# Swapping which token half leads at the layer barriers of a two-layer hybrid encoder step

## The chip, the cores and the metric

One core of one Trainium2 chip runs the whole program. The metric is device time in microseconds (us) of one execution; the times of several executions are given as a median. "The profile" is one execution, recorded by the hardware profiler. Engines are named PE (TensorE, its matmuls; PEld its weight loads), DVE (VectorE), ACT (ScalarE), POOL (GpSimd) and SP (SyncE, whose queue issues nearly all DMAs here).

## The reference, cut to what matters

640 tokens (512 of a prompt and 8 x 16 of running streams) of width 1024 pass through two layers. What is around the change:

```python
x = x + rmsnorm(merged @ w_out, g_post_mix)           # end of the mixing sub-layer
f = rmsnorm(x, g_pre_ffn) @ w_gate_up
f = (silu(f[..., :2816]) * f[..., 2816:]) @ w_down
x = x + rmsnorm(f, g_post_ffn)                        # end of the layer
# next layer: h = rmsnorm(x, g_pre_mix); u = h @ w_in
```

A norm over the 1024 channels needs every output of the projection before it, and every product behind it needs the whole norm. These two places, after `w_out` and after `w_down`, are the barriers of a layer. All arithmetic is fp32: weights and activations are split into a high and a low part, and each product is three matmuls.

## The kernel before, in words

Channels lie on the 128 partitions, tokens in the free dimension. The 640 token columns are worked in two halves (`HALF`, L27): half 0 has 256 columns, half 1 has 384. A `Unit` (L218) is one output tile of 128 channels: its weights (8 tiles of 128x128 for `w_out` and `w_gu`, 7 for a part of `w_down`) are loaded by SP as `raw` and split by ACT (`wh`) and DVE or POOL (`wl`); POOL does it for `w_in`. `run` (L244) issues three matmuls for each weight tile on one half into a PSUM tile `pg` (four buffers, L93) and calls the unit's own evacuation. So a unit of 8 tiles has 24 matmuls in each half.

Most units run half 0 and then half 1 in a row. At a barrier this is changed by `add_halves` (L314): pass A runs all units on one half, pass B the same units on the other. The last `keep` units keep their weights from A and go first in B; the others load theirs again. `barrier` (L325) puts the eight units of `w_out`, or of the last part of `w_down`, in this order: pass A on half 0, then the norms of half 0 as a task in lane "bar", pass B on half 1, then the norms of half 1 as a task in lane "bar2". Lane "bar" is finished before the next units are issued. The units behind the barrier (twelve of `w_gu`, L1418, or twelve of `w_in`, L1402) run as two passes too: A on half 0, whose norm is finished by then, with the norms of half 1 beside it, and B on half 1; lane "bar2" is finished ahead of their first B unit.

A task is a generator whose stages are issued one at a time, about one after each unit (`pump`, L272). The norms at a barrier (`bar_mix` L1301, `bar_ffn` L1343) consist of `postnorm` (L413) and `prenorm` (L387). In order of the tiles they write:
- `cs`: PE sums the squares over channels; SP loads the eight tiles `xl` of the residual stream;
- nine small DVE instructions on 2 or 3 columns (a square root and a reciprocal, the last writes `ry`), and PE spreads the result over partitions (`rb`);
- `mo<-mo,pk,rb` and `mo<-mo,xl` (`dn` at the layer's end): eight scalings and eight additions of the residual on DVE; SP stores the eight tiles to `xd`;
- `psq`: eight squares on ACT and seven additions on DVE;
- the second `cs`, nine small instructions, second `rb`;
- `ht<-mo,pk,rb`: eight scalings on DVE; `hh` (ACT) and `hl` (DVE): the split in two parts, which the matmuls of the next units read.

The evacuation of a `w_out` unit is on ACT (L1297 and the square at L410) with an addition `acc<-acc,sq` on DVE; that of a `w_down` unit is an addition on DVE (L140) with the same square and `acc`. A gate unit of `w_gu` is evacuated by a Tanh on ACT (`ft<-pg`, L1314) and `fg<-ft,pg` on DVE (L140), an up unit by `fg<-fg,pg` on DVE and the split `fh`, `fl`. Short tiles (`xl`, `psq`, `ht`, `sq`, `acc`, `ft`, `fg`) share 11 buffers of the pool `hf` (L87).

The framework decides the final order on each engine with a timeline of its own: earlier issued instructions have priority, later ones fill gaps, so an instruction can stand a little ahead of or behind its place in the code. The engines then work their queues in this order.

There are five such places in the program: the start of layer 0 (only norms, half 0 first), the barrier after `w_out` in layers 0 and 1, the barrier between the layers, and the end of layer 1 (L1427), where pass A already runs on half 1 and B on half 0 and nothing but the last norm follows.

Of the kernel before, what the change touches and what calls it, by code (L numbers as in the profile page):

```python
# [72 lines left out]
KEEP_W = (3, 4, 4, 4)  # L73
# [3 lines left out]
def emit(tc, ctx, I, O):  # L77
# [20 lines left out]
    def nm(s):  # L98
        uid[0] += 1
        return f"{s}_{uid[0]}"  # L100

    def blk(shape, s="b", dt=F32):
        return bpool.tile(shape, dt, tag="b", name=nm(s))
# [35 lines left out]
    def stt(o, a, s, b, op0, op1):  # L139
        V.scalar_tensor_tensor(o, a, s, b, op0=op0, op1=op1)  # L140
# [34 lines left out]
    def colsum(sq, n):  # L175

        ps = psb([P, 24], "cs")
        for j in range(n):
            mm(ps[:, j:j + 1], sq[:, j * P:(j + 1) * P], C["ones"], True, True)
        return ps  # L180
# [75 lines left out]
    lanes = {n: deque() for n in ("bar", "bar2", "attn", "ssd", "yn", "convp", "conv", "sc")}  # L256
# [26 lines left out]
    def flush(lane):  # L283
        stuck = 0
        while lanes[lane]:
            if step(lane) or not lanes[lane]:
                stuck = 0
                continue
            stuck += 1
            if stuck > 500:  # L290
                raise RuntimeError("lane is blocked: " + lane)
            for other in ("sc", "convp", "conv"):
                if other != lane:
                    step(other)
# [5 lines left out]
    def trim(flush_all=False):  # L300
        while pending:
            u, lag = pending[0]
            if not flush_all and len(pending) - 1 < lag:
                return
            actions.append(("B", u, 1))
            pending.popleft()
# [7 lines left out]
    def add_halves(us, keep, first=0, between=None):  # L314

        trim(True)
        for i, u in enumerate(us):
            u.drop = i < len(us) - keep
            actions.append(("A", u, first))
        if between:  # L320
            add_hook(between)
        for u in us[len(us) - keep:] + us[:len(us) - keep]:
            actions.append(("B", u, 1 - first))

    def barrier(units, keep, norms, first):  # L325

        add_halves(units, keep, 0, lambda: lanes["bar"].append(norms(0)))
        add_hook(lambda: lanes["bar2"].append(norms(1)))
        add_hook(lambda: flush("bar"))
        first.before = lambda: flush("bar2")  # L330

    def add_hook(f):
        actions.append(("H", f, None))
# [12 lines left out]
    def layer(l):  # L346
        L = {}
# [20 lines left out]
        def par(n, j):  # L368
            o = _PK[n][0]
            return L["pk"][:, o + j:o + j + 1]  # L370
# [69 lines left out]


        def ev_krdt(ps, half, c):
            if half == 0:
                L["raw0"] = blk([P, NT], "raw0")
            act(L["raw0"][:, c], ps, AF.Identity, bias=par("dt_bias", 0))

# [81 lines left out]

        def ev_lora(key, j, n, gname):
            def ev(ps, half, c):  # L530
                if half == 0:
                    L[key, j] = blk([P, NT], key)
                nc.scalar.copy(L[key, j][:, c], ps)
                sq_acc(key, j, half, ps)
                if j == n - 1:
                    if half == 0:
                        L[key + "n"] = [(blk([P, NT], key + "h", F32R), blk([P, NT], key + "l", F32R)) for _ in range(n)]
                    lanes["bar" if n == 2 else "bar2"].append(task_lora(key, n, gname, half))
            return ev

        def task_lora(key, n, gname, half):
            c, nch = HALF[half], HCH[half]
            for _ in range(YL):
                yield
            ps = colsum(L.pop(("sq", key, half)), nch)
            yield
            y = rsqrt(ps, nch, 1.0 / (n * P))
            yield
            rb = bcast(y, nch)
            for j in range(n):  # L550
                t = L[key, j]
                stt(t[:, c], t[:, c], par(gname, j), rb, ALU.mult, ALU.mult)
                split(L[key + "n"][j][0][:, c], L[key + "n"][j][1][:, c], t[:, c])
            if half == 1 and key == "lat":

                lown = lpool.tile([P, 2, P], F32, tag="lown", name=nm("lown"))
                for j in range(n):
                    dma(O["lat"][l, j], L[key, j])
                    G.tensor_copy(lown[:, j, :], L[key, j][:, SEQ:])
                L["lown"] = lown  # L560
            yield
# [284 lines left out]

        def ev_glu_b(j):
            def ev(ps, half, c):
                if half == 0:
                    L["pp", j] = blk([P, 30 + SEQ], "pp")  # L850
                    L["sp", j] = hf(NB * (30 + DS), "sp").rearrange("p (b t) -> p b t", b=NB)
                    G.memset(L["pp", j][:, :30], 0.0)
                    dma(L["sp", j][:, :, :30], I["state_conv"][l, j])
                pp, sp = L["pp", j], L["sp", j]
                t = hf(HW[half], "gt")
                act(t, ps, AF.Tanh, scale=0.5)
                a = L["ga", j, half]

                if half == 0:
                    stt(pp[:, 30:286], t, 1.0, a, ALU.add, ALU.mult)  # L860
                else:
                    stt(pp[:, 286:542], t[:, :256], 1.0, a[:, :256], ALU.add, ALU.mult)
                    stt(sp[:, :, 30:], t[:, 256:].rearrange("p (b t) -> p b t", t=DS), 1.0,
                        a[:, 256:].rearrange("p (b t) -> p b t", t=DS), ALU.add, ALU.mult)
            return ev
# [423 lines left out]

        def wout(m):  # L1290
            def ev(ps, half, c):
                if half == 0:
                    if m == 0:
                        L["mo"] = [None] * 8
                    L["mo"][m] = blk([P, NT], "mo")

                nc.scalar.mul(L["mo"][m][:, c], ps, 0.5)  # L1297
                sq_acc("mo", m, half, ps, 0.5)
            return Unit(I["w_out"][l, m], 8, lambda k: L["mg"][k], ev)

        def bar_mix(half):  # L1301
            sq = yield from postnorm("mo", L["mo"], half, "g_post_mix", xin, xd)
            if half == 0:
                new_h()
            yield
            yield from prenorm(L["mo"], sq, half, "g_pre_ffn")
# [4 lines left out]
        def gu(j):  # L1311
            def ev_g(ps, half, c):
                t, f = hf(HW[half], "ft"), hf(HW[half], "fg")
                act(t, ps, AF.Tanh, scale=0.5)  # L1314
                stt(f, t, 1.0, ps, ALU.add, ALU.mult)
                L["fg", j, half] = f

            def ev_u(ps, half, c):
                if half == 0:
                    L["f", j] = (blk([P, NT], "fh", F32R), blk([P, NT], "fl", F32R))  # L1320
                f = L["fg", j, half]
                tt(V, f, f, ps, ALU.mult)
                split(L["f", j][0][:, c], L["f", j][1][:, c], f)
            return [Unit(I["w_gu"][l, 2 * j], 8, h_rhs, ev_g), Unit(I["w_gu"][l, 2 * j + 1], 8, h_rhs, ev_u)]
# [18 lines left out]
        def bar_ffn(half):  # L1343
            sq = yield from postnorm("dn", L["dn"], half, "g_post_ffn", xd, O["y"] if last else xd, not last)
            if not last:
                nxt = layers[l + 1]
                if half == 0:
                    nxt["load_params"]()
                    nxt["new_h"]()
                yield  # L1350
                yield from nxt["prenorm"](L["dn"], sq, half, "g_pre_mix")
# [26 lines left out]
        def schedule():  # L1378
# [12 lines left out]
            def z(g):  # L1391
# [3 lines left out]
            first = ([wu("krdt", ev_krdt, done_krdt)]  # L1395
                     + [wu(f"kv{j}", ev_lora("lat", j, 2, "g_kv")) for j in range(2)]
                     + [wu(f"q{j}", ev_lora("uq", j, 3, "g_q")) for j in range(3)] + glu(0) + g1[:4])
            if l == 0:
                barrier([], 0, first_norm, first[-KEEP_W[0]])
            else:  # L1400
                barrier([layers[l - 1]["down"](2, m) for m in range(8)], KEEP_W[3], layers[l - 1]["bar_ffn"], first[-KEEP_W[0]])
            add_halves(first, KEEP_W[0])  # L1402
            add_units(g1[4:5])
            add_hook(lambda: (flush("bar"), flush("bar2")))
            add_units([k_unit(p) for p in range(4)] + [VUnit(I["w_uv"][l], 2, None, None)])
# [9 lines left out]
            add_units([mix_ssm(m) for m in range(8)])  # L1415
            us = [u for j in range(6) for u in gu(j)]
            barrier([wout(m) for m in range(8)], KEEP_W[1], bar_mix, us[-KEEP_W[2]])
            add_halves(us, KEEP_W[2])  # L1418
            for g in range(3):
                for j in GROUPS[g]:  # L1420
                    if j >= 6:
# [19 lines left out]
    done = 0  # L1441
# [3 lines left out]
    for i, (k, u, half) in enumerate(actions):  # L1445
# [3 lines left out]
        if i in pos:  # L1449
            for n in loads[done:pos[i] + 3]:  # L1450
                actions[n][1].load()
            done = max(done, pos[i] + 3)
# [163 lines left out]
```

## Time and profile before

| what | value |
|---|---|
| median of 3 runs | 2757.91 us (2756.06 to 2759.37) |
| the profiled execution's own time | 2758.69 us |
| its span, first to last instruction | 2756.9 us |
| mean granted clock of TensorE | 0.983 of full speed |
| PE busy | 2654.8 us, 96% of the span |
| DVE / ACT / POOL busy | 56% / 40% / 29% |

The span is what the engines' records cover; 1.8 us of the execution's own time lie around it. Matmuls overlap one another in the records, so a busy PE is one that has matmuls in flight; what is lost there shows as PE idle time and as time at the lower clock.

### The profile page before, as it was taken

To read this page: it belongs to the slowest core of one execution; us is meant where nothing else is said; L and a number is where in the kernel's file an instruction comes from. 1 tells how busy PE (TensorE), PEld (TensorE's weight loads), DVE (VectorE), ACT (ScalarE), POOL (GpSimd) and SP (SyncE) were. 2 spreads that over 40 slices of the span, in tenths; PEclk is the share of its full clock that TensorE was granted. 3 is DMA by queue.
4 is the path that set the end of the run, shared out by engine and by line. 5 is a ranking of instruction groups with operands and counts; after the bars stand their busy time and mean duration, and the time that the engine had idled before them with its cause. 6 is when DMAs were issued, how large, how long until landed. Compare 5 with 4: busy or idle time off the path is not lost. (4 is left out here: it accounts for less than half of the span.)

```text
span 2756.9 us, 47456 instructions
## 1 busy us (share of the span) xinstructions
PE 2654.8 (96%) x17652; PEld 2563.2 (93%) x17652; DVE 1550.5 (56%) x3382; ACT 1092.5 (40%) x2437; POOL 812.4 (29%) x796
## 2 busy tenths in 40 slices
PE   7999998999999899999999899999999998999998
PEld 7999887899999899999989899888999998999997
DVE  6364758565476732333674648676555666323336
ACT  5535453443334432222455354544433344322222
POOL 5554553544430000000055544645544200000000
PEclk9999999999999999999999999999999999999999
DMA  6443242534644422222454433344436344322224
GB/s 185 148 150 105 74 133 92 157 118 133 210 150 134 161 80 74 74 80 72 128 179 145 137 92 103 114 132 134 141 115 224 122 153 131 91 74 69 81 73 130
DMA packets 248536, 337.81 MB, mean 123 GB/s; under 512 B 52464, under 2 KB 139056, under 8 KB 248304
## 3 DMA queue, kind: packets, MB, share of 16 engines
q1 hardware_dynamic: 246720, 333.75, 39.1%
q8 instruction: 139, 2.28, 0.3%
q10 hardware_dynamic: 1584, 1.02, 0.1%
q14 instruction: 93, 0.76, 0.1%
HBM read 268.73 MB, written 65.94 MB: 121 GB/s over the span
## 5 line engine op out<-in xcount | busy, mean ns | idle before, releaser
L121 PE MATMUL pg<-hh,wh 128*128 128x256 f32 (+1 forms) x3296 | 1045.7, 318 | 26.9 <-DVE fg L140 18.2
L121 PE MATMUL pg<-hl,wh 128*128 128x256 f32 (+1 forms) x3296 | 1038.4, 315 | 5.1 <-DVE hl L137 5.1
L121 PE MATMUL pg<-hh,wl 128*128 128x256 f32 (+1 forms) x3296 | 1029.6, 313 | 0.0
L137 POOL TENSOR_TENSOR wl<-raw,wh 128x512 fp32r<-128x512 f32 (+2 forms) x364 | 513.0, 1415 | 1171.0 <-ACT wh L143 1124.5
L143 ACT CAST wh<-raw 128x512 fp32r<-128x512 f32 (+1 forms) x696 | 423.6, 610 | 850.1 <-PE pg L121 749.9
L121 PEld LDWEIGHTS pg<-hh,wh 128*128 128x128 f32 x3296 | 628.4, 191 | 36.5 <-DVE fg L140 18.6
L121 PEld LDWEIGHTS pg<-hl,wh 128*128 128x128 f32 x3296 | 628.2, 191 | 13.8 <-DVE hl L137 6.0
L121 PEld LDWEIGHTS pg<-hh,wl 128*128 128x128 f32 x3296 | 627.8, 191 | 6.0 <-issue 4.0
L137 DVE TENSOR_TENSOR wl<-raw,wh 128x512 fp32r<-128x512 f32 x332 | 224.3, 677 | 337.8 <-ACT wh L143 336.1
L121 PE MATMUL pg<-fh,wh 128*128 128x256 f32 (+1 forms) x648 | 200.4, 310 | 0.0
L121 PE MATMUL pg<-fl,wh 128*128 128x256 f32 (+1 forms) x648 | 200.3, 309 | 0.0
L121 PE MATMUL pg<-fh,wl 128*128 128x256 f32 (+1 forms) x648 | 200.2, 309 | 0.0
L140 DVE SCALAR_TENSOR_TENSOR cv<-pp,pk,cv 128x512 f32<-128x512 f32 x184 | 157.3, 855 | 2.6 <-POOL cv L137 2.6
L121 PEld LDWEIGHTS pg<-fh,wl 128*128 128x128 f32 x648 | 121.9, 188 | 0.0
L121 PEld LDWEIGHTS pg<-fl,wh 128*128 128x128 f32 x648 | 121.9, 188 | 0.0
L121 PEld LDWEIGHTS pg<-fh,wh 128*128 128x128 f32 x648 | 121.8, 188 | 0.0
L140 DVE SCALAR_TENSOR_TENSOR sa<-pd,pk,sa 128x664 f32<-128x664 f32 x96 | 104.9, 1092 | 20.3 <-ACT sa L985 19.5
L137 POOL TENSOR_TENSOR cv<-cv,cvt 128x640 f32<-128x640 f32 x56 | 88.9, 1587 | 81.8 <-ACT cvt L896 72.0
L140 DVE SCALAR_TENSOR_TENSOR cv<-sp,pk,cv 128x128 f32<-128x128 f32 x184 | 93.2, 506 | 0.0
L137 DVE TENSOR_TENSOR fg<-fg,pg 128x256 f32<-128x256 f32 (+1 forms) x88 | 42.7, 487 | 83.7 <-PE pg L121 83.4
L143 ACT CAST fh<-fg 128x256 fp32r<-128x256 f32 (+1 forms) x88 | 40.3, 460 | 111.6 <-DVE fg L137 108.5
L137 DVE TENSOR_TENSOR acc<-acc,sq 128x256 f32<-128x256 f32 (+1 forms) x96 | 59.9, 625 | 37.0 <-ACT sq L410 35.4
(307 smaller groups left out, 4419.2 us busy)
## 6 DMA issues: line engine op xcount, KB each, us to landing
raw<-in_w_in SPq DMA_DIRECT2D x284, 256.0 KB, 2.8
raw<-in_w_gu SPq DMA_DIRECT2D x208, 256.0 KB, 2.7
raw<-in_w_down SPq DMA_DIRECT2D x72, 256.0 KB, 2.7
raw<-in_w_mix SPq DMA_DIRECT2D x64, 256.0 KB, 3.1
ma<-gd SPq DMA_DIRECT2D x48, 320.0 KB, 4.1
raw<-in_w_out SPq DMA_DIRECT2D x48, 256.0 KB, 2.9
gd<-gs SPq DMA_DIRECT2D x48, 192.0 KB, 2.3
hb<-in_state_ssm SPq DMA_DIRECT2D x64, 128.0 KB, 3.3
```

The source lines that it names most:

```text
L121: nc.tensor.matmul(ps, l, r, start=a, stop=b)
L137: eng.tensor_tensor(o, a, b, op=op)
L140: V.scalar_tensor_tensor(o, a, s, b, op0=op0, op1=op1)
L143: nc.scalar.copy(hi, src)
```

## The change

At the two `w_out` barriers and at the barrier between the layers, pass A now runs on half 1 (384 columns) and pass B on half 0 (256 columns); the norms of half 1 come first and those of half 0 second, and the two passes of the units behind the barrier are turned round in the same way. The start of layer 0 keeps its order by an argument, and the end of layer 1 had the new order already. The other edits make buffers be allocated by whichever half comes first.

```diff
-    def barrier(units, keep, norms, first):
+    def barrier(units, keep, norms, first, lead=1):
 
-        add_halves(units, keep, 0, lambda: lanes["bar"].append(norms(0)))
-        add_hook(lambda: lanes["bar2"].append(norms(1)))
+        add_halves(units, keep, lead, lambda: lanes["bar"].append(norms(lead)))
+        add_hook(lambda: lanes["bar2"].append(norms(1 - lead)))
...
         def ev_krdt(ps, half, c):
-            if half == 0:
+            if "raw0" not in L:
                 L["raw0"] = blk([P, NT], "raw0")
...
-                if half == 0:
+                if (key, j) not in L:
                     L[key, j] = blk([P, NT], key)
...
-            if half == 1 and key == "lat":
+            L[key, "done"] = L.get((key, "done"), 0) + 1
+            if L[key, "done"] == 2 and key == "lat":
...
-                if half == 0:
-                    if m == 0:
-                        L["mo"] = [None] * 8
+                if "mo" not in L:
+                    L["mo"] = [None] * 8
+                if L["mo"][m] is None:
                     L["mo"][m] = blk([P, NT], "mo")
...
             sq = yield from postnorm("mo", L["mo"], half, "g_post_mix", xin, xd)
-            if half == 0:
+            if half == 1:
                 new_h()
...
-                if half == 0:
+                if half == 1:
                     nxt["load_params"]()
                     nxt["new_h"]()
...
-                barrier([], 0, first_norm, first[-KEEP_W[0]])
+                barrier([], 0, first_norm, first[-KEEP_W[0]], 0)
...
-            add_halves(first, KEEP_W[0])
+            add_halves(first, KEEP_W[0], 0 if l == 0 else 1)
...
-            add_halves(us, KEEP_W[2])
+            add_halves(us, KEEP_W[2], 1)
```

## Rows read from the trace of the kernel before

**Rows 1.** The page, part 1: busy time of each engine.

```profile
PE 2654.8 (96%) x17652; PEld 2563.2 (93%) x17652; DVE 1550.5 (56%) x3382; ACT 1092.5 (40%) x2437; POOL 812.4 (29%) x796
```

**Rows 2.** Waits of PE: total us, times, longest us.

```profile
PE pg L121 <- DVE fg L140: 18.2, 2, 9.1
...
PE pg L121 <- DVE hl L137: 5.1, 4, 1.7
...
PE pg L121 <- ACT sq L410: 2.5, 1, 2.5
```

**Rows 3.** Windows, first `w_out` barrier: pass B to restart, then the pass behind.

```profile
core 0: us, PE busy (x) PEld busy (x) DVE busy (x) ACT busy (x) POOL busy (x), PEclk, DMA share, GB/s
861.34:898.57 37.23, 35.79 (x213) 35.59 (x211) 24.16 (x67) 17.84 (x43) 0.00 (x0) 1.00 0.42 128
898.57:916.81 18.24, 18.24 (x153) 18.04 (x153) 14.15 (x37) 7.96 (x16) 0.00 (x0) 1.00 0.64 217
916.81:925.90 9.09, 0.00 (x0) 0.00 (x0) 9.09 (x20) 4.80 (x11) 0.00 (x0) 0.73 0.78 260
925.90:932.00 6.10, 6.10 (x32) 6.10 (x32) 3.80 (x10) 2.10 (x5) 0.00 (x0) 0.56 0.35 121
```

**Rows 4.** Windows, second `w_out` barrier: the stall in the pass behind it.

```profile
2279.79:2288.89 9.10, 0.00 (x1) 0.01 (x1) 9.10 (x20) 5.63 (x13) 0.00 (x0) 0.67 0.78 259
```

**Rows 5.** Windows, barrier between the layers: A, B to restart, then `w_in` pass A.

```profile
1328.46:1348.61 20.15, 20.15 (x170) 20.15 (x170) 14.65 (x30) 11.45 (x23) 0.00 (x0) 1.00 0.62 183
1348.61:1386.76 38.15, 34.00 (x193) 33.39 (x192) 27.22 (x73) 16.22 (x35) 7.74 (x6) 0.94 0.45 141
...
1406.77:1409.31 2.54, 0.00 (x0) 0.00 (x0) 2.54 (x5) 2.54 (x8) 1.39 (x1) 0.97 1.00 361
1409.31:1431.04 21.73, 21.68 (x169) 21.50 (x170) 20.90 (x46) 13.66 (x31) 16.20 (x13) 0.93 0.65 197
```

**Rows 6.** ScalarE and VectorE around the first stall: start, us, engine, operation.

```profile
921.47 2.17 ACT L382 ACTIVATE psq<-mo 128x384 f32<-128x384 f32 x5
...
925.44 0.74 DVE L140 SCALAR_TENSOR_TENSOR fg<-ft,pg 128x256 f32<-128x256 f32 x2
```

**Rows 7.** End of layer 1, 384 columns first: pass A's window, then the chain's timeline.

```profile
2691.13:2720.76 29.63, 29.63 (x171) 29.63 (x171) 16.45 (x30) 12.06 (x23) 0.00 (x0) 1.00 0.58 171
...
2725.57 0.72 PE L121 MATMUL cs<-c_ones,acc 128*128 128x1 f32 x6
...
2729.44 0.18 DVE L194 RECIPROCAL ry<-rt 128x3 f32<-128x3 f32 x1
...
2731.90 0.83 PE L121 MATMUL rb<-c_ident,ry 128*128 128x128 f32 x6
...
2732.77 4.29 DVE L140 SCALAR_TENSOR_TENSOR dn<-dn,pk,rb 128x384 f32<-128x384 f32 x8
```

**Rows 8.** DVE groups by form, 898.57 to 946 us: the norm of 384 columns.

```profile
L137 DVE TENSOR_TENSOR mo<-mo,xl 128x384 f32<-128x384 f32 x8 | 4.2, 551 | 0.0
L137 DVE TENSOR_TENSOR psq<-psq,psq 128x384 f32<-128x384 f32 x7 | 3.6, 549 | 0.0
```

**Rows 9.** DVE groups by form, 861.34 to 898.57 us: beside pass B.

```profile
L137 DVE TENSOR_TENSOR wl<-raw,wh 128x512 fp32r<-128x512 f32 x9 | 6.2, 689 | 7.3 <-ACT wh L143 7.3
L137 DVE TENSOR_TENSOR acc<-acc,sq 128x384 f32<-128x384 f32 x6 | 3.3, 554 | 1.1 <-ACT sq L410 0.9
...
L140 DVE SCALAR_TENSOR_TENSOR ht<-mo,pk,rb 128x256 f32<-128x256 f32 x8 | 3.2, 476 | 0.4 <-PE rb L121 0.4
...
L137 DVE TENSOR_TENSOR mo<-mo,xl 128x256 f32<-128x256 f32 x8 | 2.8, 417 | 0.0
```

**Rows 10.** Timeline of PE, between the layers: the second sum and its spreading.

```profile
1378.08 0.50 PE L121 MATMUL cs<-c_ones,psq 128*128 128x1 f32 x4
1381.85 1.20 PE L121 MATMUL rb<-c_ident,ry 128*128 128x128 f32 x4 [2.46 <-DVE ry L194]
```

**Rows 11.** DVE groups by form, 1386.76 to 1413 us, between the layers.

```profile
L137 DVE TENSOR_TENSOR dn<-dn,xl 128x384 f32<-128x384 f32 x8 | 7.4, 988 | 0.0
```

More of the change, by code (lines that the diff above doesn't have):

```diff
@@ L535, in ev @@
                 if j == n - 1:
-                    if half == 0:
+                    if key + "n" not in L:
                         L[key + "n"] = [(blk([P, NT], key + "h", F32R), blk([P, NT], key + "l", F32R)) for _ in range(n)]
@@ L848, in ev @@
             def ev(ps, half, c):
-                if half == 0:
+                if ("pp", j) not in L:
                     L["pp", j] = blk([P, 30 + SEQ], "pp")
@@ L1302, in bar_mix @@
             sq = yield from postnorm("mo", L["mo"], half, "g_post_mix", xin, xd)
-            if half == 0:
+            if half == 1:
                 new_h()
@@ L1318, in ev_u @@
             def ev_u(ps, half, c):
-                if half == 0:
+                if ("f", j) not in L:
                     L["f", j] = (blk([P, NT], "fh", F32R), blk([P, NT], "fl", F32R))
@@ L1346, in bar_ffn @@
                 nxt = layers[l + 1]
-                if half == 0:
+                if half == 1:
                     nxt["load_params"]()
```

## The prediction

> **What bounds the kernel now.** I read the page first: TensorE is busy for 96% of the span [rows 1], so the change can only win or lose in the time when it is not, and in time at the lower clock. PE's waits come next: the largest wait of matmuls that stands at the places of this change is the one for `fg`, 18.2 us in two pieces; `hl` has 5.1 us, `sq` one piece of 2.5 us [rows 2]. The windows put them on the barriers.
>
> At a `w_out` barrier pass B (384 columns) and the restart behind it take 37.23 us [rows 3]. At the end of layer 1 a pass of 168 matmuls of 384 columns takes 29.63 us [rows 7], 0.176 us each, so 192 take 33.9 us; only 3.3 us of the 37.23 are not matmuls of that pass (four short sums and spreadings, and the wait for `hl`). The norm of the 256-column half is hidden. The loss comes behind it: after 18.24 us of the next pass TensorE stands for 9.09 us, and 9.10 us in the other layer [rows 3, 4]. There the norm of the 384-column half holds DVE and ACT: the Tanh that frees PSUM waits behind `psq` on ACT, and `fg` comes at 925.44 us [rows 6]. With four PSUM buffers full, PE stops. The clock falls: the 6.10 us behind the stall ran at a mean granted clock of 0.56, which is 2.7 us lost [rows 3].
>
> [...]
>
> **The change part by part.** No instruction is added or removed; per layer the same columns, splits, loads and norms run. Two things are swapped: which norm lies in which cover, and how long the covers are. The three moved places are the two `w_out` barriers and the one between the layers. All terms are against the profiled execution, 2758.69 us (span 2756.9 and 1.8 around it); the median is 0.8 us lower.
>
> *The second norm gets 384-column cover.* In the pass behind the barrier PE ran 144 matmuls (six units) before it stopped. At 0.176 us these last 25.4 us, where they took 18.24 us with the sums between them. The stall ended 27.3 us after the restart (925.90 less 898.57, [rows 3]). The norm of 256 columns is shorter: 23 DVE instructions of the burst lose some 0.134 us each (551 against 417 ns, [rows 8, 9]), 3.1 us, so PSUM is freed about 24.2 us after the restart, ahead of the 25.4 us. I take the whole 9.09 and 9.10 us as gone, and between the layers the 2.54 us with its 1.5 us of clock, since there too six units pass before the wait.
>
> *The first norm loses its cover.* It now runs 384 columns beside a pass B of 256. That pass lasts 20.15 us for 168 matmuls [rows 5], so 23.0 us for 192. The end of layer 1 has this order already and gives the first part of the chain: from the end of pass A at 2720.76 us to `rb` at 2731.90 us are 11.1 us, and 0.9 us more to the first scaling [rows 7]. Then DVE has 4.3 us of scalings [rows 7], 4.2 us of additions and 3.6 us of square sums [rows 8]: 12.1 us. Between them stand weight splits and `acc`: in today's pass B 6.2 and 3.3 us in 37.23 us [rows 3, 9], a quarter of the time. The bounds are none and 3.1 us; I take 2.0, nearer to the upper one, because B units now follow each other faster. From the second sum to its spreading I take the 3.8 us between the layers, where PE idles too [rows 10], and from there to the restart 4.9 us (1381.85 to 1386.76, [rows 5, 10]) and 1.1 us for eight longer scalings (4.29 against 3.2 us, [rows 7, 9]). Sum: 11.1 + 0.9 + 12.1 + 2.0 + 3.8 + 6.0 = 35.9 us from the end of pass A to the restart.
>
> At `w_out` this is 12.9 us beyond the matmuls of pass B, where it was 3.3: 9.6 us lost against 9.1 won, +0.5 us at each barrier. The half-clock stretch behind the stall I leave as it is, since one stall of this length takes the place of another; it may move by 2 us either way. Between the layers it is 15.8 us against 8.5, 7.3 us lost against 2.5 and 1.5 won: +3.3 us. In all 2 x 0.5 + 3.3 = +4.3 us: 2763.0 on the profiled execution, 2762.2 beside the median; I say 2762.
>
> *Edits costed at nothing.* Pass A at `w_out` now begins with the half that the units before it finished last. At the end of layer 1 the same turn exists and its window is busy throughout, 29.63 of 29.63 us [rows 7]; if the cover is too short, the last tile's split is late by one or two DVE instructions, about 1 us a barrier. On SP the `xl` loads and `xd` stores of the first norm are larger, and raw weights of the next units are queued behind stores that wait for DVE; their units cannot start before the restart anyway, so the stall hides that, and without that cover it would cost a few us more. The B passes behind the barriers (256 columns now) reload weights for most units: DVE needs two splits of 0.69 us [rows 9] and its evacuation in some 2.8 us of a unit, and today's pass A does the same at this width. In the `w_in` units POOL splits; today's pass A of 256 columns has PE busy for 21.68 of 21.73 us beside it [rows 5].
>
> [...] Between the layers the residual additions of 384 columns took 988 ns each, against 551 ns behind `w_out`, where POOL is idle [rows 8, 11]; POOL was busy for 16.20 of 21.73 us in the window behind [rows 5]. [...]
>
> **The rivals.** *The first norm's chain is shorter than its parts* (faster). In the last barrier `ry` was ready at 2729.62 us, 2.3 us before `rb` was issued [rows 7]: the order on PE held it back. If the new order doesn't, if nothing breaks into the burst (2.0) and if the second sum takes only its short instructions (some 2.5 instead of 3.8), each chain loses 5.6 us, three times 16.8: 2745. Half of it gives 2753.6. For it: the unused 2.3 us. Against it: DVE has weight splits to do in any pass B.
>
> *The second norm still stalls* (slower). The margin above is 1.2 us. It decides at the point where the second norm's squares end more than 25.4 us after the restart. DVE may owe work by then: the nine splits (6.2 us, [rows 9]) compete with a longer first norm. With 5 us more, PE stands for 3.8 us and loses 2.7 us of clock at both `w_out` barriers: +13.0, 2775. For it: the thin margin. Against it: `acc` of the second half is complete long before the restart, so its sum can start early.
>
> *POOL stands in the way of the first norm between the layers* (slower). If the 15 two-input instructions of the burst are each stretched by the 0.44 us of [rows 8, 11], that is +6.6, about 2769. Against it: the `w_in` splits start mostly when pass B has given its buffers back.
>
> That the change does nothing is hardly possible: the columns of the `w_out` and `w_down` passes tell at once whether the order turned.
>
> **How the numbers follow.** The forecast has a chance of 0.43, the shorter chain 0.22, the second stall 0.25, POOL 0.10. A measurement of this kernel can tell about 0.2% from no change, 5.5 us: the bounds are 2752.4 and 2763.4 us. The forecast's own range, from the bounds of the interruptions (-2 to +1.1 us, three times), is 2756 to 2766, and two thirds of it lie within the upper bound. So slower: 0.25 + 0.10 + about a third of 0.43, less the mild ends of both, 0.40; faster 0.20, the shorter chain but for its mild end; the same 0.40. The range reaches half way into the shorter chain and takes in the second stall: 2750 to 2776.
>
> **What would show it.** Right: no wait for `fg` any more; instead, at each of the three barriers, a stall of about 10 us ahead of the restart, split by the second sum and its spreading, with the half clock behind it; 35.9 us from the end of pass A to the restart. Wrong: a restart less than 31 us after pass A (the first rival), a wait for `fg` or `sq` in the pass behind (the second), or additions of `dn` well over 551 ns in the first norm (the third). The forecast falls as a whole if a stall appears away from the three barriers.

## The result, and the profile after

The changed kernel took 2775.99 us (median of 6 runs, 2774.59 to 2779.43) against 2757.79 us for the kernel before (6 runs, 2755.24 to 2760.19): a ratio of 1.0068, interval 1.0055 to 1.0081, 18.2 us slower. The forecast was 2762, 4.3 us slower; the time lies at the very end of the range. The profiled execution took 2774.59 us with a span of 2772.8 us, 15.9 us more than before.

The page's busy times and PE's waits (total us, times, longest us) of the changed kernel, to be laid beside [rows 1, 2]:

```profile
PE 2658.1 (96%) x17652; PEld 2565.5 (93%) x17652; DVE 1560.6 (56%) x3382; ACT 1091.1 (39%) x2437; POOL 817.7 (29%) x796
```

```profile
PE rb L121 <- DVE ry L194: 29.2, 11, 8.9
...
PE cs L121 <- DVE psq L137: 10.3, 3, 7.6
PE pg L121 <- ACT sq L410: 7.9, 2, 4.1
PE cs L121 <- DVE acc L137: 7.1, 5, 2.2
...
PE pg L121 <- DVE hl L137: 2.3, 1, 2.3
PE dte L121 <- DVE dth L502: 2.2, 1, 2.2
```

The 18.2 us of `fg` are gone, as forecast. In their place stand `psq` (7.6 us once), `sq` (3.7 and 4.1 us), more of `acc` and `ry`, and a small one that was forecast nowhere: `dte` waits 2.2 us for `dth`. (These belong to the `dt` task, which computes the step sizes of the state-space part in small DVE operations of 80 columns, `dth` among them, and sums them in short matmuls, `dte`.) DVE does the same 3382 instructions in 10.1 us more.

**Where the time went.** Three stretches of the program hold the whole change. Each runs from the first matmul of one pass to the first of another: from `w_out` to the last `w_down` part (in each layer), and from there to the next `w_out`. In windows of the changed kernel they are:

```profile
838.59:1330.54 491.95, 483.24 (x3257) 482.19 (x3257) 219.79 (x437) 163.65 (x328) 0.00 (x0) 0.98 0.31 95
...
1330.54:2214.71 884.17, 846.72 (x5565) 801.67 (x5565) 562.39 (x1251) 381.88 (x888) 413.64 (x396) 0.98 0.44 136
...
2214.71:2706.53 491.82, 481.74 (x3258) 480.71 (x3257) 219.81 (x437) 163.31 (x328) 0.00 (x0) 0.99 0.31 95
```

And of the kernel before:

```profile
838.57:1328.46 489.89, 479.35 (x3258) 478.95 (x3257) 218.75 (x437) 163.50 (x328) 0.00 (x0) 0.99 0.31 96
...
1328.46:2201.31 872.85, 847.38 (x5565) 802.34 (x5565) 553.45 (x1251) 383.45 (x888) 410.52 (x396) 0.98 0.44 137
...
2201.31:2691.13 489.82, 479.29 (x3258) 478.88 (x3258) 218.55 (x437) 163.49 (x328) 0.00 (x0) 0.99 0.31 96
```

The two `w_out` stretches grew by 2.1 and 2.0 us, the one that holds the barrier between the layers by 11.3; 0.5 us lie behind the last. That is the 15.9. The second column says how: at `w_out` PE stood *less* (491.95 less 483.24 is 8.7 us, before 10.5; 10.1 and 10.5 in the other layer) and was busy longer for the same matmuls, by 3.9 and 2.5 us. Between the layers PE was busy as long as before and stood 37.5 us instead of 25.5.

**The first `w_out` barrier.** Its windows: pass A, pass B to the restart, and then pieces of the second.

```profile
838.59:872.40 33.81, 33.81 (x195) 33.81 (x195) 14.82 (x24) 14.79 (x30) 0.00 (x0) 1.00 0.38 118
872.40:911.51 39.11, 30.40 (x223) 29.35 (x223) 28.90 (x70) 19.45 (x44) 0.00 (x0) 0.85 0.46 155
...
890.70:894.49 3.79, 0.06 (x2) 0.01 (x1) 3.79 (x10) 3.79 (x11) 0.00 (x0) 0.80 0.89 319
894.49:897.50 3.01, 3.01 (x14) 3.01 (x15) 3.01 (x9) 1.03 (x4) 0.00 (x0) 0.50 0.32 121
897.50:900.74 3.24, 3.24 (x20) 3.24 (x20) 1.70 (x5) 1.30 (x4) 0.00 (x0) 0.65 0.26 79
...
907.12:910.67 3.55, 1.32 (x3) 0.84 (x4) 3.55 (x8) 3.47 (x7) 0.00 (x0) 0.50 0.00 1
910.67:917.00 6.33, 6.33 (x21) 6.33 (x22) 4.99 (x17) 0.07 (x1) 0.00 (x0) 0.51 0.01 3
```

The stall is in pieces, and the clock is low behind them. After the first 3.8 us PE runs at a granted clock of 0.50, then 0.65, so it works off pass B slowly; after the later ones it runs 6.33 us at 0.51. Busy time by what the clock withheld: 1.5 + 1.1 + 0.7 + 3.1 = 6.4 us, where the one stall before cost 2.7 [rows 3]. The difference, 3.7, is nearly the 3.9 us of longer busy time. The piece in pass B comes from ACT; PE's timeline, then ACT's, and the last square sum on DVE:

```profile
882.95 0.83 PE L121 MATMUL rb<-c_ident,ry 128*128 128x128 f32 x6
...
894.49 0.58 PE L121 MATMUL pg<-mgh,wh 128*128 128x256 f32 x1 [3.73 <-ACT sq L410]
...
900.74 0.72 PE L121 MATMUL cs<-c_ones,psq 128*128 128x1 f32 x6
```

```profile
891.99 2.17 ACT L382 ACTIVATE psq<-mo 128x384 f32<-128x384 f32 x5
894.07 1.19 ACT L410 ACTIVATE sq<-pg 128x256 f32<-128x256 f32 x4
```

```profile
897.01 0.55 DVE L137 TENSOR_TENSOR psq<-psq,psq 128x384 f32<-128x384 f32 x1
```

ACT squares the eight tiles of the first norm with one evacuation between them, and the squares that free pass B's PSUM tiles stand behind them: what ACT did to `fg` before [rows 6] it now does to pass B. The second column sum (`cs`) then queues on PE behind the delayed matmuls: it starts at 900.74 us, though DVE finished `psq` at 897.6 us.

**Between the layers.** Windows of pass A, pass B, the wait for the second sum, and up to the restart:

```profile
1330.54:1360.15 29.61, 29.61 (x171) 29.61 (x171) 16.39 (x30) 12.25 (x23) 0.00 (x0) 1.00 0.43 125
1360.15:1381.39 21.24, 21.23 (x180) 21.03 (x179) 17.28 (x39) 9.35 (x19) 5.45 (x4) 1.00 0.63 207
1381.39:1389.02 7.63, 0.00 (x0) 0.03 (x1) 7.63 (x13) 3.33 (x9) 4.53 (x3) 0.70 0.59 184
1389.02:1398.94 9.92, 5.00 (x19) 4.36 (x19) 7.43 (x23) 4.09 (x8) 0.00 (x0) 0.50 0.15 42
```

Pass A to restart takes 68.4 us, before 58.3 [rows 5]: 10.1 us lost, forecast 7.3. Pass B itself never waits. In the 7.63 us without a matmul DVE is busy throughout, and POOL is busy for 4.53 of them. DVE's groups by form from 1360.15 to 1398.94 us (busy us, mean ns):

```profile
L137 DVE TENSOR_TENSOR psq<-psq,psq 128x384 f32<-128x384 f32 x7 | 6.1, 909 | 0.0
L137 DVE TENSOR_TENSOR dn<-dn,xl 128x384 f32<-128x384 f32 x8 | 4.8, 644 | 0.0
...
L137 DVE TENSOR_TENSOR acc<-acc,sq 128x256 f32<-128x256 f32 x7 | 4.0, 575 | 0.4 <-ACT sq L410 0.2
```

Seven additions of squares took 909 ns each, against 549 behind `w_out` [rows 8]. The two `w_in` passes behind the restart (288 matmuls each), changed and before:

```profile
1398.94:1500.51 101.57, 97.96 (x645) 96.80 (x646) 64.64 (x152) 47.88 (x108) 56.55 (x43) 0.95 0.46 136
```

```profile
1386.76:1487.44 100.68, 98.08 (x649) 96.85 (x650) 62.27 (x152) 51.04 (x111) 54.81 (x44) 0.96 0.47 146
```

They take 0.9 us more, where the forecast had 4.0 less. The rest of the stretch is 714.2 us, before 713.9.

### The profile page after: what moved, and what is told of

The parts are those of the page before. It is cut to its first block, busy times and chain, and to the rows that moved or that the text cites. A ratio compares the mean times of both kernels' runs of the same rounds, so it can differ in the third digit from the quotient of the medians.

```text
span 2772.8 us, 47468 instructions
## 1 busy us (share of the span) xinstructions
PE 2658.1 (96%) x17652; PEld 2565.5 (93%) x17652; DVE 1560.6 (56%) x3382; ACT 1091.1 (39%) x2437; POOL 817.7 (29%) x796
## 4 chain that ended last, share of the span: by engine, by line
PE 79%; DVE 13%; DMA 3%; issue 2%; ACT 1%; POOL 0%; SPq 0%; DVEq 0%; ACTq 0%; POOLq 0%
PE pg L121 67%; DVE cv L140 6%; PE op L121 1%; PE sc L121 1%; PE yo L121 1%; PE dp L121 1%; PE sps L121 1%; PE yp L121 1%; PE rb L121 1%; DVE sa L140 1%; PE ops L121 1%; PE ss L121 1%; DVE ht L140 1%; PE tp L661 1%; DVE psq L137 1%
## 5 line engine op out<-in xcount | busy, mean ns | idle before, releaser
L121 PE MATMUL pg<-hh,wh 128*128 128x384 f32 (+1 forms) x3296 | 1047.8, 318 | 9.6 <-ACT hh L143 4.1
L121 PE MATMUL pg<-hl,wh 128*128 128x384 f32 (+1 forms) x3296 | 1039.0, 315 | 2.3 <-DVE hl L137 2.3
L121 PE MATMUL pg<-hh,wl 128*128 128x384 f32 (+1 forms) x3296 | 1030.7, 313 | 0.0
L137 POOL TENSOR_TENSOR wl<-raw,wh 128x512 fp32r<-128x512 f32 (+2 forms) x364 | 520.8, 1437 | 1171.7 <-ACT wh L143 1116.8
L121 PEld LDWEIGHTS pg<-hl,wh 128*128 128x128 f32 x3296 | 625.8, 190 | 10.7 <-issue 4.5
L121 PE MATMUL pg<-fl,wh 128*128 128x384 f32 (+1 forms) x648 | 201.1, 310 | 0.0
L121 PE MATMUL pg<-fh,wl 128*128 128x384 f32 (+1 forms) x648 | 201.0, 310 | 0.0
L121 PE MATMUL pg<-fh,wh 128*128 128x384 f32 (+1 forms) x648 | 201.0, 311 | 0.0
```

What stands on the lines that cost most here:

```text
L121: nc.tensor.matmul(ps, l, r, start=a, stop=b)
L137: eng.tensor_tensor(o, a, b, op=op)
```

## The experiments

Two measures are used. One is the ratio to the kernel before. The other is the length of the three stretches in the profile, found as above; it keeps what happens at a barrier apart from the rest. Where nothing was changed between the layers, the middle stretch was 870.0 to 872.9 us long in three profiles (before, changed at `w_out` only, additions on POOL), so it scatters by at least 3 us.

| kernel | median us | ratio (interval) | `w_out`, layer 0 | middle | `w_out`, layer 1 |
|---|---|---|---|---|---|
| before | 2757.79 | 1 | 489.9 | 872.9 | 489.8 |
| changed | 2775.99 | 1.0068 (1.0055 to 1.0081) | 492.0 | 884.2 | 491.8 |
| changed, again | 2775.73 | 1.0065 (1.0051 to 1.0080) | 492.3 | 880.3 | 492.5 |
| changed at `w_out` only | 2764.18 | 1.0017 (1.0008 to 1.0025) | 492.9 | 870.0 | 492.5 |
| changed between layers only | 2770.46 | 1.0041 (1.0025 to 1.0056) | 490.1 | 886.5 | 489.6 |
| changed, low parts on ACT | 2770.02 | 1.0044 (1.0031 to 1.0058) | 492.8 | 874.4 | 491.5 |
| changed, low parts left out | 2771.81 | 1.0055 (1.0041 to 1.0069) | 492.3 | 878.1 | 491.8 |
| changed, `dt` stage later | 2778.92 | 1.0075 (1.0057 to 1.0093) | 491.0 | 886.3 | 492.9 |
| changed, `dt` behind a pass | 2770.49 | 1.0038 (1.0026 to 1.0050) | 492.8 | 880.5 | 493.2 |
| both of these left out | 2769.30 | 1.0033 (1.0020 to 1.0046) | 491.2 | 873.7 | 492.8 |
| before, running squares | 2757.56 | 0.9998 (0.9987 to 1.0009) | 490.9 | 871.9 | 487.1 |
| before, five PSUM buffers | 2782.50 | 1.0083 (1.0070 to 1.0096) | 487.1 | 892.2 | 487.9 |
| before, additions on POOL | 2755.43 | 0.9986 (0.9977 to 0.9995) | 489.4 | 871.1 | 488.8 |

Each ratio is to runs of the kernel before on the same chip; their medians were 2755.98 to 2759.61 us. It is estimated over all runs and can differ a little from the quotient of two medians. One more kernel, with finer stages, stands in its own paragraph.

**The two halves of the change, each alone.** At `w_out` only:

```diff
...
-                barrier([layers[l - 1]["down"](2, m) for m in range(8)], KEEP_W[3], layers[l - 1]["bar_ffn"], first[-KEEP_W[0]])
-            add_halves(first, KEEP_W[0], 0 if l == 0 else 1)
+                barrier([layers[l - 1]["down"](2, m) for m in range(8)], KEEP_W[3], layers[l - 1]["bar_ffn"], first[-KEEP_W[0]], 0)
+            add_halves(first, KEEP_W[0], 0)
```

> Only the two w_out barriers lead with 384 columns; the barrier between the layers leads with 256 as before. Theory (the barrier between the layers bears the loss): 2757.8 + 1.4 + 2.0, about 2761 us, 2758 to 2764. Rival (all three barriers lose alike, 6 us each, through longer first norms and the half clock): about 2770.

Between the layers only:

```diff
...
-            barrier([wout(m) for m in range(8)], KEEP_W[1], bar_mix, us[-KEEP_W[2]])
-            add_halves(us, KEEP_W[2], 1)
+            barrier([wout(m) for m in range(8)], KEEP_W[1], bar_mix, us[-KEEP_W[2]], 0)
+            add_halves(us, KEEP_W[2], 0)
```

> Only the barrier between the layers leads with 384 columns. Theory: 2757.8 + 11 to 14, 2769 to 2772 us, with the stalls behind both w_out barriers (9.1 us for fg) back. Rival (all three alike): about 2764.

(In both, the norm that allocates the next tiles is turned as well.) Measured: +4.7 us (interval 2.2 to 6.9) at the two `w_out` barriers, +11.3 us (6.9 to 15.4) between the layers, each from its ratio. The second median lies in the range of the theory, the first just above it (2764.18); the barriers don't lose alike. The forecast had +1.0 and +3.3: both terms were too small. In the second kernel `fg` is back with 18.2 us, and the 7.6 us wait for `psq` and the 2.2 us for `dth` are there: both belong to the barrier between the layers.

**POOL: low parts written by ACT.** The first three `w_in` units of layer 1 get their low part from ACT, so POOL has nothing to split beside the norm.

```diff
...
+        if eng == "zero":
+            nc.scalar.copy(hi[:, :w], raw[:, :w])
+            nc.scalar.mul(lo[:, :w], raw[:, :w], 0.0)
...
```

> The changed kernel, but the low parts of the first three w_in units of layer 1 (first load) are written by ScalarE as zeros, so POOL is idle beside the first norm between the layers; that part of the product is left out. Theory (POOL's splits stretch the norm's two-input instructions): psq additions back from 909 to about 550 ns, residual additions from 644 to 551, the restart 3 to 5 us earlier, 2771 to 2773 us. Rival (the short cover alone): durations may fall but the time stays within 1 us of 2776, because the next wait takes over.

The additions went back to 554 ns (`psq` and `dn`) and 423 ns (`acc`). The wait for `psq` fell only from 7.63 to 5.9 us, because ACT now had the eight squares and the extra writes to do and DVE waited 1.3 us for it. The restart came 1.8 us earlier, not 3 to 5. The ratio is 1.0044, below the changed kernel. The run shows the stretching of the instructions, but not its price, since the edit brought a cost of its own.

**POOL: low parts left out.** The same units use the high part in the place of the low one; ACT does nothing extra.

```diff
...
+        if eng == "hi":
+            nc.scalar.copy(hi[:, :w], raw[:, :w])
+            lo = hi
...
```

> The changed kernel, but the first three w_in units of layer 1 use their high parts in place of the low ones (first load): the six splits on POOL beside the first norm between the layers are left out, with nothing on another engine instead; their low product is left out. Theory (an exclusive use by POOL stretches the two-input instructions of the norm by 4.1 us of busy time): the wait of TensorE for psq falls from 7.6 to 3 to 5 us, the time by 3 to 5 us against the changed kernel. Rival (the norm is bound by ScalarE's squares and the queue order, not by POOL): the wait stays above 6 us, the time within 2 us of the changed kernel.

DVE's groups by form at this barrier (1355.89 to 1394.12 us), and the second sum and the restart in PE's timeline:

```profile
L137 DVE TENSOR_TENSOR dn<-dn,xl 128x384 f32<-128x384 f32 x8 | 4.0, 550 | 0.0
L137 DVE TENSOR_TENSOR psq<-psq,psq 128x384 f32<-128x384 f32 x7 | 3.6, 548 | 0.0
...
L137 DVE TENSOR_TENSOR acc<-acc,sq 128x256 f32<-128x256 f32 x7 | 2.9, 421 | 0.4 <-ACT sq L416 0.2
```

```profile
1384.20 1.41 PE L121 MATMUL cs<-c_ones,psq 128*128 128x1 f32 x6 [4.29 <-DVE psq L137]
...
1394.12 0.69 PE L121 MATMUL pg<-hl,wh 128*128 128x384 f32 x1 [2.34 <-DVE hl L137]
```

The additions take 550, 548 and 421 ns again, where they took 644, 909 and 575. Pass A began at 1329.07, so to the restart it takes 65.05 us; it was 68.4 us in the changed kernel, in its repeat and in the kernel changed between the layers only. The wait fell from 7.63 to 4.29. Both say 3.3 us, and the chain from the end of pass A is 35.4 us, where the forecast had 35.9. POOL's splits were the part missing in the chain, and their price is 3.3 us. In medians the kernel is 3.9 us under the repeat of the changed one on the same chip (2771.81, 2775.73), though the two intervals overlap.

**The same kernel again**, for the scatter.

> The changed kernel, unaltered, as the standard for the next two on the same chip: ratio 1.005 to 1.008 to the kernel before, as measured.

The ratio repeats, 1.0065. The middle stretch was 880.3 instead of 884.2 us: differences of 4 us there between single profiles are not evidence, while the 68.4 us up to the restart repeat to 0.02 us and the 101.6 us of the two passes behind it as well. The scatter lies behind these: a wait of PE for a load (`qlp` for `al`) is 6.9 us in all in one profile's middle stretch and 3.9 in the other's, and one of 3.5 us (`tps` for `ps`) is missing in the second.

**The new wait for `dth`.** First the stage that starts this work was put off by one step in layer 1:

```diff
-            for _ in range(YDT):
+            for _ in range(YDT + l):
```

> The changed kernel with the second stage of the dt task of layer 1 (dte) issued one unit later. Theory (a new wait of 2.2 us with 1.7 us of clock behind it has eaten what was won behind the restart): no wait for dth, 3 to 4 us faster than the changed kernel. Rival (the splits on POOL slow the whole 256-column pass, and the wait only shows it): another wait of 1.5 to 2.5 us appears in the same pass, under 1 us faster.

The framework's timeline put the instructions at the same place; the wait of 2.2 us stayed. The ratio of 1.0075 tells nothing on the question. Then the whole task was started from a hook behind a later unit of layer 1:

```diff
...
-            lanes["ssd"].append(task_dt())
+            if l == 0:
+                lanes["ssd"].append(task_dt())
...
+            if l == 1:
+                add_hook(lambda: lanes["ssd"].append(task_dt()))
```

> The changed kernel; in layer 1 the dt task (dtp, dth, dte) starts behind the two passes of the first w_in units instead of within pass B. Theory (its wait of 2.2 us and 1.7 us of clock behind it are a new loss of the 256-column pass): no wait for dth in pass B, 2 to 4 us faster than the changed kernel's 2775.7. Rival (the wait has a cause that moves with it): the same wait in the next units, within 1.5 us of the changed kernel.

No wait for `dth` is left in pass B, and the ratio is 1.0038 where the changed kernel and its repeat had 1.0068 and 1.0065: 7 to 8 us, or 5 by the medians as they stand. The two passes behind the restart now take 95.8 us instead of 101.6:

```profile
1398.73:1494.53 95.80, 94.36 (x627) 93.26 (x628) 53.36 (x123) 46.86 (x104) 56.24 (x43) 0.97 0.50 145
```

The wait and the half clock behind it (3.40 us at 0.50 from 1486.90 us, 1.7 us) make 3.9 of these 5.8; the other 1.9 are the task's own 18 matmuls, which now stand later. In the whole middle stretch the gain is 3.7 us against the changed kernel and none against its repeat, within its scatter. That the place costs time is shown by the passes and the ratios; how much of the 7 to 8 us is this wait is not.

**Both left out.** No low parts in three units and the task behind the pass:

> The changed kernel with both: no POOL splits beside the first norm between the layers (high parts in place of low ones in three units), and the dt task of layer 1 behind the passes. Theory: what is left of the loss between the layers is what was forecast for it, 3 to 4.5 us, so the time is 2767 to 2769 us. Rival (a further cause between the layers): 2771 or more.

The middle stretch is 873.7 us, 0.9 more than before, against 880.3 to 886.5 us in the four profiles that have both costs (changed, again, between layers only, `dt` stage later). That alone proves little: with low parts on ACT and the task in its old place it was 874.4. The ratio is 1.0033; less the 1.0017 of the `w_out` part, 0.0016 or 4.4 us remain for this barrier, where the forecast had 3.3. So the two causes account for what the forecast missed between the layers, within the scatter. (2769.30 is just above the theory's range; the kernel before was at 2759.61 us on this chip.)

**Is it the order or the amount of work that makes the old stall?** Three edits of the kernel before. A running sum, so that each square is added as soon as it is there:

```diff
...
+            acc = hf(HW[half], "psq")
+            act(acc, xs[0][:, HALF[half]], AF.Square)
+            for k in range(1, 8):
+                r = hf(HW[half], "psq")
+                act(r, xs[k][:, HALF[half]], AF.Square)
+                tt(V, acc, acc, r, ALU.add)
...
```

> The kernel before, with the eight squares of a norm added to one running sum (7 additions as before, 2 or 3 short buffers instead of 8). If the fg stall of 9.1 us at the w_out barriers is one of short buffers held by psq, it shrinks to under 5 us and the time falls by 8 to 15 us, to 2743 to 2750. If it is the order of the queues on ScalarE and VectorE, the stall stays at 8 to 10 us and the time within 3 us of 2757.8.

`fg` fell from 18.2 us to 10.7 us in four pieces, and the time didn't move (0.9998). In layer 1 the `w_out` stretch won 2.7 us, in layer 0 it lost 1.0. The stall shrank, nearly as the one theory said, and the time stood still, as the other said, so this decides for neither. Then smaller stages for the second norm, its lane at twice the rate (`slow_squares` is the running sum with a pause in it):

```diff
-    rate = dict(bar=2.0, bar2=2.0, attn=RATE[0], ssd=RATE[1], yn=RATE[5], convp=RATE[2], conv=RATE[3], sc=RATE[4])
+    rate = dict(bar=2.0, bar2=4.0, attn=RATE[0], ssd=RATE[1], yn=RATE[5], convp=RATE[2], conv=RATE[3], sc=RATE[4])
...
-                r = squares(tiles, half) if sq else None
+            if half == 1 and key == "mo":
+                r = yield from slow_squares(tiles, half)
+            else:
+                r = squares(tiles, half) if sq else None
...
```

> The kernel before, with the second norm of the w_out barriers issued in smaller stages (two tiles at a time, running squares, twice the rate), so that gate units' evacuations stand between them. If the queue order is what holds fg, the two 9.1 us stalls fall below 3 us in all and the clock behind them stays up: 2735 to 2745 us. If the amount of VectorE work in that stretch is the bound, a stall of the same total comes back at the end of the pass: within 5 us of 2757.

2780.67 us, 1.0085 (1.0068 to 1.0103). PE's waits from 900 to 1000 us:

```profile
PE pg L121 <- DVE fg L140: 8.7, 2, 4.7
PE pg L121 <- DVE hl L137: 1.4, 1, 1.4
PE rb L121 <- DVE ry L194: 0.8, 1, 0.8
```

Without `hl`, which was there before, 9.5 us in three pieces in place of 9.1 in one; 10.6 in layer 1. The two `w_out` stretches took 494.3 and 493.4 us, 4.5 and 3.6 more than before: standing as long in pieces, PE was busy 4.1 and 2.1 us longer. The doubled rate also cost time far from these barriers (13.2 us ahead of the first), so the ratio is no measure of the stages. Neither theory had these stretches longer. Last, a fifth PSUM buffer, taken from the other work:

```diff
-    psg = pool("psg", 4, space=bass.MemoryType.PSUM)
-    psb_ = pool("psb", 4, space=bass.MemoryType.PSUM)
+    psg = pool("psg", 5, space=bass.MemoryType.PSUM)
+    psb_ = pool("psb", 3, space=bass.MemoryType.PSUM)
```

> The kernel before with five PSUM buffers for the units and three for the short work (four and four). TensorE can run one unit of 256 columns more, 2.8 us, before the stall for fg: the two stalls fall from 9.1 to 6 to 6.5 us, 5 to 7 us faster, 2750 to 2753, if three buffers are enough for the short work. Rival: the short work waits for its buffers elsewhere and takes the gain back, 2757 or more.

The stalls fell to 7.4 and 7.5 us and the `w_out` stretches by 2.8 and 2.0 us, but the middle one grew by 19.4, as the rival said: short matmuls there waited longer (once 6.1 us, `tp` for `p`), and these had one buffer less; that each such wait is one for a buffer isn't shown. So the number of buffers bears on the length of the stall, and none can be spared here. What bounds it, order or amount, the three edits leave open.

**A faster version.** During the old stall DVE is busy for 9.09 of 9.09 us, and POOL is idle there [rows 3]. In the kernel before, four of the eight residual additions of the second norm were put on POOL:

```diff
-                tt(V, t, t, xs[k], ALU.add)
+                tt(G if key == "mo" and half == 1 and k % 2 else V, t, t, xs[k], ALU.add)
```

> The kernel before, with four of the eight residual additions of the second norm at the w_out barriers on POOL, which is idle there. If the amount of VectorE work sets the fg stall, it falls by about 2 us at each barrier, 2752 to 2755. If POOL and VectorE exclude each other, POOL's additions (1 us or more each) hold VectorE's weight splits and square sums, and the stall stays at 9 us or grows: 2757 to 2762.

2755.43 us (10 runs) beside 2759.61 (21 runs), 0.9986 (0.9977 to 0.9995): slightly faster than both kernels, 3.9 us under the one before. PE's wait, and DVE's timeline beside POOL's additions:

```profile
PE pg L121 <- DVE fg L140: 17.1, 2, 8.5
```

```profile
915.99 2.08 DVE L137 TENSOR_TENSOR wl<-raw,wh 128x512 fp32r<-128x512 f32 x2
```

Each stall is only 0.6 us shorter (8.5 for 9.1), though DVE has 2.2 us of additions less. Two weight splits took 2.08 us beside POOL, 0.7 more than alone (0.69 each [rows 9]), and in DVE's order five additions of `psq` now stand ahead of `fg` where four stood. So both halves of the expectation hold in part, and the amount of work on DVE isn't all that sets the stall. The `w_out` stretches are 0.5 and 1.0 us shorter; the rest of the 3.9 is spread over the run, within the scatter of its parts.

## Why the prediction was right and wrong

**Right: the old stalls go, the first norm's stall takes their place.** No wait for `fg` or for `sq` in the pass behind a barrier is left, so the second rival (0.25) didn't happen; that its 2775 us lies beside the measured time is chance. No restart came under 31 us after pass A, so the first didn't happen either. The first `rb` came 10.6 and 11.2 us after pass A, forecast 11.1. Pass A on the late half was busy throughout (33.81 of 33.81, 29.61 of 29.61), and PE waits for no load at the barriers: two of the edits costed at nothing cost PE nothing directly.

**At `w_out`, +2.0 each instead of +0.5: the step that failed is "one stall of this length takes the place of another", and with it the chain's sum, which put a hold on pass B at nothing.** The stall is in pieces, not one. In layer 0 PE stood 1.8 us less and was busy 3.9 us longer, in layer 1 0.5 less and 2.5 longer. The chain of 39.1 us (forecast 35.9; 39.7 in layer 1) is longer for the same reason: pass B stood 3.7 us for ACT's squares and ran on at a clock of 0.50, then 0.65, and the second sum queued behind it on PE. Up to the last square sum the chain took 25.2 us, where the forecast had 26.1 (11.1 + 0.9 + 12.1 + 2.0); then `cs` came 3.2 us late (900.74 less 897.56), a term put at nothing; from there to the restart it was 10.8 instead of 9.8. Of the 6.4 us of clock some 2.7 lie behind the restart, as before; the rest lies ahead of it, within this chain. Against the longer chain, the stretch behind the restart won 10.9 us (419.0 instead of 429.9), not 9.1. The prediction had costed pass B's weight reloads, but not a hold on its PSUM. That ACT's order holds these buffers is read from the timelines of both layers (3.7 and 4.1 us for `sq`); it wasn't tried by an edit. Between the layers, where DVE empties the PSUM tiles, pass B doesn't stand.

**Between the layers, the larger error: +11.3 instead of +3.3.** Two steps failed. (The 8.5 us of the sum are the 38.15 us of pass B and the restart [rows 5] less the 29.63 us of a pass of 168 matmuls of this width [rows 7].)

The first is the term for POOL, which was left out of the sum and given 0.10 as the third rival, on the ground that "the `w_in` splits start mostly when pass B has given its buffers back". They did start mostly then, four of six from 1378.49 us; but the norm's square sums ran at that very time, from 1381.96 us on. POOL was busy for 5.45 of pass B's 21.24 us and 4.53 of the 7.63 us wait. The rival's price of 6.6 us, 15 instructions at 0.44, was an upper bound: the seven square sums paid 0.36 us each (909 less 549), the additions 0.09 (644 less 551), 3.3 us together. Taking POOL's work away gave back 3.3 us of chain, and 35.4 us remain of 38.8. The rest of the chain had been sized right, as a sum.

The second is the 2.5 us of wait and 1.5 us of clock entered as won behind the restart. (The 1.5 us are 7% of the 21.73 us at a mean granted clock of 0.93 [rows 5]; in that trace the first 3.69 of them ran at 0.56 and the rest at 1.00.) The wait for `sq` [rows 5] is gone, but the two passes behind the restart took 101.6 us, before 100.7: 4.9 us worse than forecast. With the 2.9 us by which the chain was longer, that is nearly all of the 8.0 us missed here. What is late next was not named: the pass behind now has units of 256 columns, and in it six of the small operations of the `dt` chain on DVE take 1.17 to 1.34 us beside POOL's splits, instead of 0.20 to 0.24, where three did before (1.25 to 1.29 us). The chain took 11.0 us from its first `dth` to its last instead of 8.1, so `dte` comes 2.2 us late and has 3.40 us at a clock of 0.50 behind it; two column sums wait 0.4 and 1.1 us. With the task moved, two operations were stretched so, the chain took 6.0 us and the passes 95.8. The prediction's own sign that it falls as a whole, a stall away from the three barriers, is this wait.

**What stays open.** Single profiles of the middle stretch differ by 4 us with the same code, so the share of `dth` in the 7 to 8 us of its experiment is not settled. The wait for `tps` of 3.5 us, 1.4 at most before, is not the change's: in the repeat of the changed kernel it is 1.1 us at most. The hold on pass B at `w_out` and what bounds the old stall were not separated by an edit.

## What to carry to other kernels

Swapping which norm is covered moved the stall here rather than removing it; count the work of the engines that empty PSUM against the cover on both sides before turning the order. Price a stall by its pieces: here the clock fell both inside pass B (0.50, then 0.65) and again at the restart (0.51), so a stall in pieces cost 6.4 us of clock where one of the same length had cost 2.7. And when a chain is moved beside another engine's work, compare the times at which both actually run: here the square sums that met POOL's splits took 909 ns each instead of 549; put as a helper where it was idle, that engine saved a little (3.9 us of 2759.6).

## What the runs showed of the hardware

A VectorE operation with one tensor input took longer beside POOL's splits too. DVE's timeline of the changed kernel, beside five splits that POOL ran from 1476.71 us for 6.76 us:

```profile
1476.43 0.20 DVE L493 TENSOR_SCALAR dth<-dth 128x80 f32<-128x80 f32 x1
1476.66 0.24 DVE L137 TENSOR_TENSOR dth<-dth,dts 128x80 f32<-128x80 f32 x1
1476.94 1.17 DVE L493 TENSOR_SCALAR dth<-dth 128x80 f32<-128x80 f32 x1
1478.15 1.26 DVE L137 TENSOR_TENSOR dth<-dth,dts 128x80 f32<-128x80 f32 x1
...
1479.66 1.29 DVE L493 TENSOR_SCALAR dth<-dth 128x80 f32<-128x80 f32 x1
```

`dth<-dth`, 0.20 us just before, took 1.17 and 1.29 us beside the splits, about as long as one of them (6.76 us for five here, 1.29 us each at the barrier of the kernel before). Of this chain six operations took 1.17 to 1.34 us in the changed kernel, and three 1.25 to 1.29 us in the kernel before. POOL's splits took longer as well, beside two-input operations of DVE: POOL's six splits at the barrier took 1.69 us each in the changed kernel (the two from 1367.95 us 2.55 together, the four from 1378.49 us 7.43) and 1.29 before:

```profile
L137 POOL TENSOR_TENSOR wl<-raw,wh 128x512 fp32r<-128x512 f32 x6 | 10.0, 1691 | 556.4 <-ACT wh L143 556.4
```

Two operations with one operand in PSUM took no longer. DVE's timeline at the barrier, beside four splits that POOL ran from 1378.49 us for 7.43 us:

```profile
1381.62 0.41 DVE L140 SCALAR_TENSOR_TENSOR dn<-pg,dn 128x256 f32<-128x256 f32 x1
1381.96 2.83 DVE L137 TENSOR_TENSOR psq<-psq,psq 128x384 f32<-128x384 f32 x2
1384.71 0.41 DVE L140 SCALAR_TENSOR_TENSOR dn<-pg,dn 128x256 f32<-128x256 f32 x1
```

The evacuations from PSUM (`pg`) take 0.41 us, as with POOL idle (a mean of 418 ns for seven in pass A of the kernel before); the two additions between them, both operands in SBUF, take 2.83 us instead of 1.1 (549 ns each [rows 8]). The two kinds differ in their operation as well as in the place of their operands, and no run separates these.
